# One decoder layer in one kernel: high-part and low-part matmuls in separate runs

## The chip, the cores and the metric

The kernel runs on one core of a Trainium2 chip. A core has five engines that run side by side, each with its own instruction queue. TensorE (PE) multiplies matrices: a weight load puts a stationary 128x128 tile into its array, and a matmul then streams a moving tile of up to 512 columns past it and adds the products into a bank of PSUM, the accumulator memory. VectorE (DVE), ScalarE (ACT) and GpSimd (POOL) do elementwise work; SyncE (SP) issues transfers between memory (HBM) and the on-chip SBUF. The metric is the time of one execution in device microseconds, as a median over several executions. The profile shows one of them.

## The reference

One layer of a hybrid decoder over 256 tokens with 2048 features, all in float32. What matters here are its projections:

- `u = rmsnorm(h)`, then `u @ w_in` with 12,320 columns: the gate z (2048), the state-space part x, B and C (4096), its step dt (32), and q, k and v of the attention (6144);
- a causal convolution, a chunked state-space scan and a gated norm on the first part; attention with three dilations on the second;
- `concat(ssd, attention) @ w_out` (4096 to 2048), a norm and the residual;
- `w_down` of `relu(u @ w_up)^2` (2048 to 8192 and back), a norm and the residual.

The result needs nearly float32 precision, so the kernel splits each operand x into a rounded high part hi and the rest lo = x - hi, and a product a * b becomes a_hi * b_hi + a_hi * b_lo + a_lo * b_hi.

## The kernel before

A product takes its weights in blocks of KB = 2 rows of 128 by NB = 512 columns. `weights` fetches a block into a tile `raw` by a transfer from SyncE (L136), has ACT write its high part into a tile `hi` (L125) and DVE the rest into a tile `lo` (L126). There are BUFS = 5 buffers each of `hi` and `lo` and four of `raw`; the whole of it runs under a high priority, so that blocks are prepared ahead.

There are two forms of product.

- *[token, feature]* (`gemm_tokens`): the activations are stationary, the weight block's 512 columns stream. Three matmuls for each 128 tokens and 128 rows: L187 (high, high), L188 (high activation, low weight), L189 (low activation, high weight). It makes z, v, w_out, w_down and the first block of w_up.
- *[feature, token]* (`gemm_features`, with `products`): 128x128 pieces of the weight block are stationary and the activations stream. The activations lie in `u2`, where for each 128 features the high parts of the 256 tokens (`uh`) and their low parts (`ul`) are neighbours. So one matmul of the weight's high piece streams 512 columns, high and low activation together (L201), and one of the weight's low piece streams the 256 high columns only (L202). The second adds into the first half of the same PSUM bank.

A [feature, token] product makes 512 features: four banks `acc[0]` to `acc[3]`, one for 128 features, and eight blocks over the 2048 rows. In each block there are four features times two row pieces, so eight pairs of an L201 and an L202, in the order of the list given to `products`: feature by feature, and within one by row piece. Each pair is one high matmul and the low matmul of the same piece. Behind a block, `pump` lets the next bit of waiting side work (a state-space group, an attention head, a piece of hidden activations) issue its instructions.

Behind the product, `added` takes the banks out in the order of the features: ACT copies a bank's second half (L219), DVE adds the first half to it (L220). There are six banks for such accumulators, so a product that follows another has two free ones for its first two features.

Thirty products go through `gemm_features`: seven for x, B and C, eight for q and k, fifteen for w_up. The first block of B is made by `first_block`, which calls `products` itself, once for each of the 16 row pieces with the four features as list, with the transposes of x (L276) set between; its order is written out by hand, the rest is ordered by priorities.

Instructions on an engine run in their order, so the order in which `products` emits its matmuls is TensorE's own order, but for high-priority side work set between them.

Of the kernel before, what the change touches and what calls it, by code (L numbers as in the profile page):

```python
# [16 lines left out]
P = 128  # L17
# [3 lines left out]
NK = D // P  # L21
# [18 lines left out]
KB = 2  # L40
# [31 lines left out]
def hymba_layer(ctx: ExitStack, tc: tile.TileContext, x, norm_mix_pre, w_in, conv_w, conv_b, dt_bias, a_log,  # L72
                d_skip, ssm_norm_w, w_out, norm_mix_post, norm_mlp_pre, w_up, w_down, norm_mlp_post,
                consts, out):
    nc = tc.nc
# [14 lines left out]
    u2 = big.tile([P, NK, 2, S], F32R, name="u2")  # L90
    uh, ul = u2[:, :, 0], u2[:, :, 1]
# [53 lines left out]
    def weights(src, k0, c0):  # L145

        with tc.high_priority(offset=AHEAD):
            raw = fetch(src, k0, c0)
            hi, lo = parts()
            with ExitStack() as order:  # L150
                while behind:
                    order.enter_context(tc.issue_after(behind.pop().ins))
                split(hi, lo, raw)
        return hi, lo
# [4 lines left out]
    def pump(n=1):  # L159
        for _ in range(n):  # L160
            if waiting:
                work = waiting.popleft()
                if next(work, work) is not work:
                    waiting.append(work)
# [5 lines left out]
    def gemm_tokens(src, c0, acts, nk, lag=0, at_end=None, pumps=1):  # L170


        acc = [bank() for _ in range(NT)]
        held = {}
        n = nk // KB
        for i in range(n + lag):
            if i < n:
                held[i] = weights(src, i * KB, c0)
            for t, at in ((0, i), (1, i - lag)):
                if not 0 <= at < n:  # L180
                    continue
                hi, lo = held[at]
                ts = slice(t * P, (t + 1) * P)
                for j in range(KB):
                    k = at * KB + j
                    a_h, a_l, r = acts(k)
                    nc.tensor.matmul(acc[t], a_h[:, r, ts], hi[:, j], start=k == 0, stop=False)  # L187
                    nc.tensor.matmul(acc[t], a_h[:, r, ts], lo[:, j], start=False, stop=False)  # L188
                    nc.tensor.matmul(acc[t], a_l[:, r, ts], hi[:, j], start=False, stop=k == nk - 1)  # L189
                if at == n - 1 and at_end:  # L190
                    at_end(t, acc[t])
            pump(pumps)
        return acc

    def features():
        return [bank().rearrange("p (b s) -> p b s", b=2) for _ in range(4)]

    def products(acc, hi, lo, k0, order):
        for f, j in order:
            k, fs = k0 + j, slice(f * P, (f + 1) * P)  # L200
            nc.tensor.matmul(acc[f], hi[:, j, fs], u2[:, k], start=k == 0, stop=False, skip_group_check=True)  # L201
            nc.tensor.matmul(acc[f][:, 0], lo[:, j, fs], uh[:, k], start=False, stop=k == NK - 1,  # L202
                             skip_group_check=True)

    def gemm_features(src, c0):


        acc = features()
        for k0 in range(0, NK, KB):
            hi, lo = weights(src, k0, c0)  # L210
            products(acc, hi, lo, k0, [(f, j) for f in range(4) for j in range(KB)])
            pump()
        return acc

# [72 lines left out]
    def first_block():  # L287
# [22 lines left out]
        for k0 in range(0, NK, KB):  # L310
            k1, k2 = k0 + KB, k0 + 2 * KB
            if k2 < NK:
                load_x(k2)
                load(k2)
            elif k2 == NK:
                load_parameters()
            products(acc, hi, lo, k0, [(f, 0) for f in range(4)])
            if k1 < NK:
                q = turn_x(k1)
            products(acc, hi, lo, k0, [(f, 1) for f in range(4)])  # L320
            if k1 == NK:
                break
            hi, lo = parts()
            if k1 >= FINE:
                part(k1, hi, lo, slice(0, KB))
            for f in range(KB):
                behind[:] = split_x(k1, q, f)
                if k1 < FINE:
                    part(k1, hi, lo, slice(f, f + 1))
            if k0 >= 4:  # L330
                squares(k0 // KB - 2)
# [103 lines left out]
    def conv_block(c0, ft0, acc=None):  # L435

        acc = acc or gemm_features(w_in, c0)
        dst = mp.tile([P, 4, S], F32, name="cT", bufs=5)
        for b in range(2):
            added(dst[:, 2 * b:2 * b + 2], acc[2 * b:2 * b + 2])  # L440
        for b in range(2):
            pad = sp1.tile([P, 2, S + 3], F32, name="pad", bufs=2)
            nc.gpsimd.memset(pad[:, :, 0:3], 0.0)
            nc.vector.tensor_tensor(pad[:, :, 3:], dst[:, 2 * b:2 * b + 2], rbc[:, None, :].to_broadcast([P, 2, S]),
                                    op=ALU.mult)
            for f in range(2):
                ft = ft0 + 2 * b + f
                d = dst[:, 2 * b + f]
                nc.vector.tensor_scalar(d, pad[:, f, 3:], cw[:, 3, ft:ft + 1], None, op0=ALU.mult)
                for w in (2, 1, 0):  # L450
                    nc.vector.scalar_tensor_tensor(d, pad[:, f, w:w + S], cw[:, w, ft:ft + 1], d,
                                                   op0=ALU.mult, op1=ALU.add)
                nc.scalar.activation(d, d, AF.Silu, bias=cb[:, ft:ft + 1])
        return dst
# [130 lines left out]
    def queries(c0, scale):  # L585
        acc = gemm_features(w_in, c0)
        dst = mp.tile([P, 4, S], F32, name="cT", bufs=5)
        for b in range(2):
            d = dst[:, 2 * b:2 * b + 2]
            added(d, acc[2 * b:2 * b + 2])  # L590
            nc.vector.tensor_tensor(d, d, scale[:, None, :].to_broadcast([P, 2, S]), op=ALU.mult)
        return dst

    for hb in range(4):
# [10 lines left out]
        acc = gemm_tokens(w_in, COL_V + hb * NB, act_u, NK)  # L605
# [60 lines left out]
    acc = gemm_tokens(w_out, 0, part, 2 * NK)  # L666
# [9 lines left out]
    for n in range(4):  # L676
        if n:
            acc = gemm_tokens(w_out, n * NB, part, 2 * NK, *((LAG_OUT, done, 2) if n == 3 else ()))
# [24 lines left out]
    acc = gemm_tokens(w_up, 0, act_u, NK, LAG_UP, None, 2)  # L703
# [20 lines left out]
    for hf in range(2):  # L724
        for fb in range(8):
            if hf == 0 and fb == 0:
                continue
            acc = gemm_features(w_up, hf * 4096 + fb * NB)
            for b in range(2):
                r = hp.tile([P, 2, S], F32, name="r", bufs=2)  # L730
                added(r, acc[2 * b:2 * b + 2])
                nc.vector.scalar_tensor_tensor(r, r, 0.0, rbc[:, None, :].to_broadcast([P, 2, S]),
                                               op0=ALU.max, op1=ALU.mult)
                hidden(4 * fb + 2 * b, r)
        for n in range(4):
            cs = slice(n * NB, (n + 1) * NB)
            last = hf == 1 and n == 3
            acc = gemm_tokens(w_down[hf * 4096:(hf + 1) * 4096], n * NB, part, 2 * NK,
                              *((LAG_DOWN, finish) if last else ()))
            for t in range(0 if last else NT):  # L740
                if hf == 0:
                    nc.scalar.activation(mw[:, t, cs], acc[t], AF.Copy)
                else:
                    nc.vector.tensor_add(mw[:, t, cs], acc[t], mw[:, t, cs])
                    junk = hp.tile([P, NB], BF16, name="junk", bufs=2)
                    nc.scalar.activation(junk, mw[:, t, cs], AF.Square, accum_out=ssq[:, t, n:n + 1])
                    nc.gpsimd.tensor_mul(mw[:, t, cs], mw[:, t, cs], wpost2[:, cs])
            if hf == 1 and n == 2:
                first3 = [sums_but_last(ssq, t) for t in range(NT)]
# [23 lines left out]
```

## Time and profile before

| what | value |
|---|---|
| median of 3 executions | 1516.53 us (1516.21 to 1521.23) |
| the profiled execution | 1517.63 us |
| its span, first to last instruction | 1515.8 us |
| PE busy | 1501.6 us, 99% of the span, 7725 matmuls |
| DVE busy | 914.5 us, 60% |
| ACT busy | 760.5 us, 50% |
| DMA | 283.13 MB, 187 GB/s on average |
| granted TensorE clock, mean | 0.998 |

The profiled execution's own time is 1.83 us longer than its span: that is what lies before its first and behind its last instruction. Busy is the time in which an engine worked on at least one instruction. Matmuls overlap in their pipeline, so one lasts longer than its distance to the next; what a matmul costs in a stream is read from the starts of matmuls in the timeline, and not from its duration. Weight loads (PEld) run beside matmuls.

### The profile page before, as it was taken

The numbers are of one execution on the slowest core, as the hardware profiler recorded it, in microseconds if no ns is written. First come the engines' busy times: TensorE is split into PE (matmuls) and PEld (weight loads), VectorE is DVE, ScalarE is ACT, GpSimd is POOL, SyncE is SP. The second block draws the span as 40 slices with busy tenths as digits, with TensorE's granted clock in tenths as the row PEclk, the third lists the DMA queues.
The fourth block names the chain that finished last, engine by engine and source line by source line (L and its number), as shares of the span: only waits on it lengthen the run. The fifth ranks groups of instructions, "written<-read, shape, count | busy, mean of one in ns | idle before, by whom it ended". The sixth has DMA issues, their size and how long they took to land.

```text
span 1515.8 us, 20167 instructions
## 1 busy us (share of the span) xinstructions
PE 1501.6 (99%) x7725; PEld 1277.5 (84%) x7725; DVE 914.5 (60%) x1314; ACT 760.5 (50%) x1065; POOL 56.7 (4%) x73
## 2 busy tenths in 40 slices
PE   9999999999999999999999999999999999999997
PEld 8888888888888888888878888888888888888885
DVE  5888897876555555544457656644444665555544
ACT  6575575554545454534456555543444555544432
POOL 0002200220000000000000000000000000000000
PEclk9999999999999999999999999999999999999999
DMA  7665666556665665576556666666566767655553
GB/s 256 195 210 180 182 181 194 177 157 181 169 178 169 175 171 174 169 267 193 185 166 215 187 183 187 187 194 194 193 192 187 191 184 187 187 193 193 192 172 125
DMA packets 147842, 283.13 MB, mean 187 GB/s; under 512 B 11313, under 2 KB 14241, under 8 KB 147233
## 3 DMA queue, kind: packets, MB, share of 16 engines
q1 hardware_dynamic: 143312, 272.37, 60.1%
q10 hardware_dynamic: 4432, 9.48, 1.8%
q8 instruction: 60, 0.98, 0.3%
q14 instruction: 38, 0.30, 0.1%
HBM read 279.68 MB, written 2.13 MB: 186 GB/s over the span
## 4 chain that ended last, share of the span: by engine, by line
PE 97%; DMA 1%; DVE 1%; issue 0%; ACT 0%; POOL 0%; POOLq 0%; DVEq 0%; SPq 0%; ACTq 0%
PE acc L201 30%; PE acc L187 16%; PE acc L189 16%; PE acc L188 16%; PE acc L202 15%; PE ps L516 1%; PE ps L559 0%; PE ps L581 0%; DMA raw_dt<-in_w_in_dram 0%; DMA raw<-in_w_in_dram 0%; DMA xs<-in_x_dram 0%; PE ps L472 0%; PE ps L582 0%; PE ps L558 0%; DVE h L646 0%
## 5 line engine op out<-in xcount | busy, mean ns | idle before, releaser
L126 DVE TENSOR_TENSOR lo<-raw,hi 128x1024 fp32r<-128x1024 f32 (+1 forms) x514 | 630.5, 1228 | 530.2 <-ACT hi L125 521.2
L125 ACT ACTIVATE hi<-raw 128x1024 fp32r<-128x1024 f32 (+1 forms) x514 | 542.1, 1056 | 651.0 <-PE acc L189 333.5
L201 PE MATMUL acc<-u,hi 128*128 128x512 f32 x1984 | 713.5, 403 | 0.0
L202 PE MATMUL acc<-u,lo 128*128 128x256 f32 x1984 | 557.2, 281 | 0.0
L201 PEld LDWEIGHTS acc<-u,hi 128*128 128x128 f32 x1984 | 373.5, 188 | 88.8 <-issue 0.2
L202 PEld LDWEIGHTS acc<-u,lo 128*128 128x128 f32 x1984 | 375.4, 189 | 1.2 <-DVE lo L126 0.3
L187 PE MATMUL acc<-hi,sh 128*128 128x512 f32 x384 | 150.6, 392 | 0.0
L187 PE MATMUL acc<-hi,ah 128*128 128x512 f32 x384 | 149.9, 390 | 0.0
L189 PE MATMUL acc<-hi,sl 128*128 128x512 f32 x384 | 149.5, 389 | 0.0
L188 PE MATMUL acc<-lo,sh 128*128 128x512 f32 x384 | 149.4, 389 | 0.0
L189 PE MATMUL acc<-hi,al 128*128 128x512 f32 x384 | 149.4, 389 | 0.0
L188 PE MATMUL acc<-lo,ah 128*128 128x512 f32 x384 | 149.4, 389 | 0.0
L187 PE MATMUL acc<-hi,u 128*128 128x512 f32 x288 | 113.0, 393 | 0.3 <-ACT u L127 0.3
L189 PE MATMUL acc<-hi,u 128*128 128x512 f32 x288 | 112.1, 391 | 0.7 <-DVE u L128 0.7
L188 PE MATMUL acc<-lo,u 128*128 128x512 f32 x288 | 112.0, 390 | 0.0
L189 PEld LDWEIGHTS acc<-hi,sl 128*128 128x128 f32 x384 | 72.1, 188 | 15.2
L189 PEld LDWEIGHTS acc<-hi,al 128*128 128x128 f32 x384 | 72.1, 188 | 15.0
L188 PEld LDWEIGHTS acc<-lo,ah 128*128 128x128 f32 x384 | 72.1, 188 | 14.9
L188 PEld LDWEIGHTS acc<-lo,sh 128*128 128x128 f32 x384 | 72.1, 188 | 14.9
L187 PEld LDWEIGHTS acc<-hi,sh 128*128 128x128 f32 x384 | 72.1, 188 | 14.8
L187 PEld LDWEIGHTS acc<-hi,ah 128*128 128x128 f32 x384 | 72.1, 188 | 14.7
L187 PEld LDWEIGHTS acc<-hi,u 128*128 128x128 f32 x288 | 54.1, 188 | 12.6 <-ACT u L127 1.5
(190 smaller groups left out, 941.0 us busy)
## 6 DMA issues: line engine op xcount, KB each, us to landing
raw<-in_w_in_dram SPq DMA_DIRECT2D x190, 512.0 KB, 3.7
raw<-in_w_up_dram SPq DMA_DIRECT2D x128, 512.0 KB, 3.8
raw<-in_w_down_dram SPq DMA_DIRECT2D x128, 512.0 KB, 3.6
raw<-in_w_out_dram SPq DMA_DIRECT2D x64, 512.0 KB, 4.3
bc<-acs_d ACTq DMA_DIRECT2D x8, 512.0 KB, 4.4
xs<-in_x_dram SPq DMA_DIRECT2D x8, 256.0 KB, 6.0
h<-in_x_dram ACTq DMA_DIRECT2D x1, 2048.0 KB, 11.7
raw<-in_w_in_dram SPq DMA_DIRECT2D x4, 256.0 KB, 5.1
```

The lines of the kernel that those rows point to most:

```text
L125: return (nc.scalar.activation(hi, src, AF.Copy), nc.vector.tensor_tensor(lo, src, hi.bitcast(F32), op=ALU.subtract))
L126: nc.vector.tensor_tensor(lo, src, hi.bitcast(F32), op=ALU.subtract))
L187: nc.tensor.matmul(acc[t], a_h[:, r, ts], hi[:, j], start=k == 0, stop=False)
L188: nc.tensor.matmul(acc[t], a_h[:, r, ts], lo[:, j], start=False, stop=False)
L189: nc.tensor.matmul(acc[t], a_l[:, r, ts], hi[:, j], start=False, stop=k == nk - 1)
L201: nc.tensor.matmul(acc[f], hi[:, j, fs], u2[:, k], start=k == 0, stop=False, skip_group_check=True)
L202: nc.tensor.matmul(acc[f][:, 0], lo[:, j, fs], uh[:, k], start=False, stop=k == NK - 1, skip_group_check=True)
L516: nc.tensor.matmul(p[:, c, r], bc[:, r, c * P:(c + 1) * P], xdt[:, c, r], start=True, stop=True)
```

## The change

`products` goes through its list twice: first all high-part matmuls (512 columns), then all low-part ones (256 columns). Its caller `gemm_features` chooses how long the list is. In the six middle blocks of the eight it passes all four features at once, so eight high matmuls come in one run and then eight low ones. In the first and the last block it calls `products` once for each feature, with two row pieces, so that each feature has two high matmuls and then two low ones. `first_block` is not edited, but its calls now make runs of four and four.

```diff
     def products(acc, hi, lo, k0, order):
+
         for f, j in order:
-            k, fs = k0 + j, slice(f * P, (f + 1) * P)
-            nc.tensor.matmul(acc[f], hi[:, j, fs], u2[:, k], start=k == 0, stop=False, skip_group_check=True)
-            nc.tensor.matmul(acc[f][:, 0], lo[:, j, fs], uh[:, k], start=False, stop=k == NK - 1,
+            nc.tensor.matmul(acc[f], hi[:, j, f * P:(f + 1) * P], u2[:, k0 + j], start=k0 + j == 0, stop=False,
                              skip_group_check=True)
+        for f, j in order:
+            nc.tensor.matmul(acc[f][:, 0], lo[:, j, f * P:(f + 1) * P], uh[:, k0 + j], start=False,
+                             stop=k0 + j == NK - 1, skip_group_check=True)
...
         for k0 in range(0, NK, KB):
             hi, lo = weights(src, k0, c0)
-            products(acc, hi, lo, k0, [(f, j) for f in range(4) for j in range(KB)])
+
+            edges = k0 in (0, NK - KB)
+            for fs in [(f,) for f in range(4)] if edges else [range(4)]:
+                products(acc, hi, lo, k0, [(f, j) for f in fs for j in range(KB)])
             pump()
```

The matmuls, their operands and their number are the same. In a middle block the first low piece is wanted eight matmuls after the first high one instead of one, and the last use of `hi` comes eight low matmuls before the block's end.

## The prediction

> **What bounds the kernel now.** I read the page first: who is busy, and what the chain that ended last is made of.
>
> ```profile
> span 1515.8 us, 20167 instructions
> PE 1501.6 (99%) x7725; PEld 1277.5 (84%) x7725; DVE 914.5 (60%) x1314; ACT 760.5 (50%) x1065; POOL 56.7 (4%) x73
> PE 97%; DMA 1%; DVE 1%; issue 0%; ACT 0%; POOL 0%; POOLq 0%; DVEq 0%; SPq 0%; ACTq 0%
> L126 DVE TENSOR_TENSOR lo<-raw,hi 128x1024 fp32r<-128x1024 f32 (+1 forms) x514 | 630.5, 1228 | 530.2 <-ACT hi L125 521.2
> L201 PE MATMUL acc<-u,hi 128*128 128x512 f32 x1984 | 713.5, 403 | 0.0
> L202 PE MATMUL acc<-u,lo 128*128 128x256 f32 x1984 | 557.2, 281 | 0.0
> L202 PEld LDWEIGHTS acc<-u,lo 128*128 128x128 f32 x1984 | 375.4, 189 | 1.2 <-DVE lo L126 0.3
> ```
>
> TensorE is busy 99% of the span and makes up 97% of the chain; the weight loads of low pieces waited for VectorE for 0.3 us in all. So there is no waiting in the [feature, token] products that a later use of `lo` could shorten. Only the rate at which matmuls follow each other can move the time. That rate is the distance between starts, since durations overlap (403 and 281 ns are longer than the distances below). So the second view is the timeline of matmuls, inside a w_up product without side work (start in us, duration, engine, line).
>
> ```profile
> 900.04 0.28 PE L202 MATMUL acc<-u,lo 128*128 128x256 f32 x1
> 900.16 0.40 PE L201 MATMUL acc<-u,hi 128*128 128x512 f32 x1
> 900.40 0.28 PE L202 MATMUL acc<-u,lo 128*128 128x256 f32 x1
> 900.52 0.40 PE L201 MATMUL acc<-u,hi 128*128 128x512 f32 x1
> 900.76 0.28 PE L202 MATMUL acc<-u,lo 128*128 128x256 f32 x1
> 900.87 0.40 PE L201 MATMUL acc<-u,hi 128*128 128x512 f32 x1
> 901.10 0.28 PE L202 MATMUL acc<-u,lo 128*128 128x256 f32 x1
> ```
>
> Three pairs take 901.10 - 900.04 = 1.06 us, or 353.3 ns a pair. Behind a low matmul the next start comes after 0.12, 0.12 and 0.11 us, behind a high one after 0.24, 0.24 and 0.23: on average 116.7 and 236.7 ns. The third view is the same timeline in a [token, feature] product, where every matmul streams 512 columns against a fresh 128x128 stationary tile, as a run of high matmuls would:
>
> ```profile
> 1400.03 0.39 PE L189 MATMUL acc<-hi,al 128*128 128x512 f32 x1
> ...
> 1406.83 0.39 PE L189 MATMUL acc<-hi,al 128*128 128x512 f32 x1
> ```
>
> Ten rounds of the three lines lie between, 30 matmuls in 6.80 us: 226.7 ns each. A matmul of 512 columns is thus 10 ns dearer where it alternates with one of 256 than where it follows its like. This is the whole room of the change, if the low matmuls do not give it back.
>
> **The change part by part.** Nothing is removed or added: 1984 high and 1984 low matmuls, each with its weight load, and the same transfers, splits and evacuations. What moves is order. Of the pairs, 30 products x 6 middle blocks x 8 = 1440 come into runs of eight, 30 x 2 end blocks x 8 = 480 into runs of two, and 64 of the first block into runs of four; the sum is the 1984 of the group's row.
>
> *Middle blocks, the high run.* Its lower end is the settled 226.7 ns. But eight are few, and the trace shows what 512-column matmuls do right behind the alternation, at the start of a w_down product that follows w_up:
>
> ```profile
> 976.36 0.28 PE L202 MATMUL acc<-u,lo 128*128 128x256 f32 x1
> 976.48 0.40 PE L187 MATMUL acc<-hi,sh 128*128 128x512 f32 x1
> 976.72 0.40 PE L188 MATMUL acc<-lo,sh 128*128 128x512 f32 x1
> 976.96 0.40 PE L189 MATMUL acc<-hi,sl 128*128 128x512 f32 x1
> 977.19 0.40 PE L187 MATMUL acc<-hi,sh 128*128 128x512 f32 x1
> ...
> 978.35 0.40 PE L189 MATMUL acc<-hi,sl 128*128 128x512 f32 x1
> ```
>
> From 976.48 to 978.35 there are eight (three rounds of the three lines, less one): 1.87 us, 233.8 ns each, and the first of them takes 0.24 us as in the alternation. The distance shrinks over a row of matmuls and not at once. That is the upper end. What comes behind a run of eight low matmuls no row shows; I take 232 ns, close to the upper end, because that row too begins behind a low matmul. Per matmul that is 4.7 ns less than 236.7.
>
> *Middle blocks, the low run.* The trace has no row of 256-column matmuls in a run with full 128x128 loads. The nearest is the dt product, 256 columns of the same `u`, run on run, with stationary tiles of half the width:
>
> ```profile
> 49.06 0.28 PE L384 MATMUL ps<-u,wdt 128*64 128x256 f32 x1
> ...
> 51.17 0.28 PE L384 MATMUL ps<-u,wdt 128*64 128x256 f32 x1
> 127.35 1.86 PEld L516 LDWEIGHTS ps<-xdt,bc 128*128 128x128 f32 x16
> 129.13 0.19 PEld L201 LDWEIGHTS acc<-u,hi 128*128 128x128 f32 x1
> ```
>
> Nine rounds of L384 and L385, 18 matmuls in 2.11 us: 117.2 ns each. The last two rows are weight loads of the full width behind each other, under matmuls of 64 columns that cannot fill the time: 16 in 1.78 us, 111.3 ns each. So a load every 117 ns is possible, though with little to spare, and though one load's record is 189 ns long. The lower end for a low run is 110 ns, the shorter of the distances shown above (0.11); the upper end is 120, the longest of them (0.12). I take the dt row's 117.2, 0.5 above the 116.7 of now.
>
> The sum for a pair in a middle block is 232 + 117.2 = 349.2 ns against 353.3: 4.1 ns less, and times 1440 it is 5.9 us. The ends are 226.7 + 110 = 336.7 (23.9 us less) and 233.8 + 120 = 353.8 (0.7 us more).
>
> One correction: the alternation is not at 353.3 everywhere. In a passage of the state-space stage it holds a faster rhythm:
>
> ```profile
> 79.97 0.40 PE L201 MATMUL acc<-u,hi 128*128 128x512 f32 x1
> ...
> 86.21 0.40 PE L201 MATMUL acc<-u,hi 128*128 128x512 f32 x1
> ```
>
> That is 18 pairs in 6.24 us, 346.7 ns. Where this holds, the runs save nothing (349.2 is 2.5 more). As an estimate, a third of the middle blocks of the seven x, B and C products is like this: 7 x 48 / 3 = 112 pairs x 6.6 ns = 0.7 us of the saving gone, which leaves 5.2 us.
>
> *End blocks.* Two high, two low: in the transition above, the first two 512-column distances are 976.72 - 976.48 = 0.24 and 976.96 - 976.72 = 0.24 us, which is the alternation's own price. I take nothing. For the range: two pairs cost 706.7 ns now, at most 2 x 240 + 2 x 120 = 720 (13 ns x 240 = 3.2 us more), at least what the middle's lower end gives, 673 (8.0 us less). The order of the features stays, so `added` finds its banks at the same times.
>
> *The first block* has 64 pairs in runs of four; at the middle's rate it is 0.3 us, which I leave out. Its first three banks end up to three high matmuls later (0.7 us); two spare banks carry the next product through its first two features, four pairs or 1.4 us, so I price this at nothing; without that cover it is 0.7 us, once.
>
> *Buffers.* `hi` is free eight low matmuls (0.94 us) earlier in a middle block, `lo` at the same time as now. The first low piece is wanted 8 x 232 ns = 1.9 us after the first high one instead of 0.24 us. Both loosen the preparation, on which TensorE hardly waits. VectorE's 1.23 us of splitting per block of 2.8 us (row L126) hides below the matmuls as before, and so does ScalarE's part. No wait is added, and nothing queues behind one. Side work is set between the same blocks.
>
> The profiled execution took 1517.6 us with 1515.8 of span and 1.8 outside; less 5.2 it is 1512.4. The median is 1.1 us below that execution, so I predict **1511.3 us** in the median's terms, 0.34% less.
>
> **The Trainium skill against this.** "TensorE: Matmul & The Clock Gate", section "Back-to-back issue gap", gives the gap of a matmul as its column count over the clock plus a constant, with no term for its neighbours. By that rule order costs nothing and the change does nothing; the trace speaks against it in part, as the same 512 columns take 226.7 ns in one place and 236.7 in the other.
>
> **The rivals.**
>
> *Order does not matter (no change, 1516.5 us).* The cost may belong to the short matmul: each of 256 columns may lay a fixed debt of 13 ns on the stream, and the next long one pays it. For it: in the transition the excess over 226.7 is paid over eight matmuls, (233.8 - 226.7) x 8 = 57 ns, though no short one came any more. Then a run of low matmuls would collect the debt, and the next high run pay it: 353.3 as before. Against: the rhythm at 346.7 shows that the same pairs can go faster. The skill's rule above ends at the same time.
>
> *The runs settle at once (about 1501 us).* The settled 226.7 with 117.2 is 343.9, 9.4 less; x 1440 = 13.5 us, and a fifth of that per pair in the end blocks, 480 x 1.9 = 0.9 us, with 0.7 taken back for the fast passages: 13.7, so 1516.5 - 13.7 = 1502.8; with low matmuls at 113 it would be 1497. For it: the neighbours within a run are all alike. Against: the slow settling in the transition.
>
> *Low runs wait for their weight loads (slower, about 1528 us).* Now every second load has a 512-column matmul to lie under. In a low run each of eight loads has only 117 ns, and the record of one is 189 ns long. If loads under 256 fp32r columns come at 130 ns, a pair is 232 + 130 = 362, 8.7 more; x 1440 = 12.5 us, 1529. If a load could only begin when the one before had ended, at 189 ns, it would be 232 + 189 - 353.3 = 67.7 x 1440 = 97 us. It decides from 353.3 - 232 = 121.3 ns per low matmul on. Against: 16 full loads in a row at 111.3 ns. For: those lay under 64-column matmuls of another type. The skill's page on TensorE, section "LDWEIGHTS (loading the stationary operand)", has 128 columns load in an estimated 107 ns; the 111.3 of this trace is near it.
>
> *The edit does not do what it says:* side work with a higher priority could split the runs, but it is set between blocks now and takes no more places than before; this would land at no change and is counted there.
>
> **How the numbers follow.** From 0.5% on (7.6 us) a measurement of this kernel can tell a change from none: below 1508.9 is faster, above 1524.1 slower. The forecast (1506 to 1515, by 230 to 233.8 for a high and 115 to 119 for a low matmul) has a chance of 0.38, and about a third of it lies beyond 0.5%; no influence of order 0.25; settling at once 0.27, all of it faster; waiting loads 0.10, nearly all slower. So faster 0.13 + 0.27 = 0.40, slower 0.09, the same 0.51. The range from 1498 to 1522 holds the forecast, no change and nearly all of the settled case, and leaves out the waiting loads (0.10) and the lower ends of the low run (0.08). Cases of gain and of no change hold most of it; the likeliest one's own range is 1506 to 1515.
>
> **What would show it.** In the timeline after: a run of eight L201 whose first distance is about 0.24 us and whose mean is near 232 ns, then eight L202 at about 117 ns; a middle block of 2.79 us instead of 2.83. High runs at 227 ns from the first on speak for settling at once; a first run of eight whose surplus equals what the low run saved speaks for the debt; L202 distances above 121 ns show waiting loads. Idle time on TensorE behind `lo` L126 or at L201 that is more than a few us in all would mean that my reading of the buffers is wrong. The prediction fails if end blocks cost more than 720 ns for two pairs, or if the rhythm of runs depends on what went before as the two rhythms of the alternation do.

## The result and the profile after

The changed kernel took 1508.89 us (median of 6, 1508.5 to 1512.54) beside 1517.25 us of the kernel before (median of 6): a ratio of 0.9944 with a 95% interval from 0.9928 to 0.9959. Run a second time, beside one of the experiments below, it gave 1509.32 us and 0.9950 [0.9936, 0.9963]. So it is 7 to 8 us faster, at and just beyond the bound of 0.5% that the prediction set. The forecast was 1511.3, a gain of 5.2 us. The granted clock is 0.998 in both profiles.

The page after, in the lines that answer to those quoted of before:

```profile
span 1507.1 us, 20168 instructions
PE 1493.2 (99%) x7725; PEld 1275.4 (85%) x7725; DVE 917.5 (61%) x1314; ACT 763.1 (51%) x1063; POOL 56.1 (4%) x73
PE 96%; DVE 2%; DMA 1%; ACT 1%; issue 1%; SPq 0%; POOL 0%; POOLq 0%; DVEq 0%; ACTq 0%
L201 PE MATMUL acc<-u,hi 128*128 128x512 f32 x1984 | 539.3, 398 | 1.3 <-DVE u L128 1.2
```

The same 7725 matmuls, TensorE still at 99%, and the span 8.7 us shorter. The low matmul's line is now L204. The first reading is the timeline inside a w_up product: one middle block. A row holds a whole run here (its start, how long it was busy, the line, the count).

```profile
1172.77 2.00 PE L201 MATMUL acc<-u,hi 128*128 128x512 f32 x8
1174.61 1.11 PE L204 MATMUL acc<-u,lo 128*128 128x256 f32 x8
1175.56 0.40 PE L201 MATMUL acc<-u,hi 128*128 128x512 f32 x1
```

Eight high matmuls take 1174.61 - 1172.77 = 1.84 us, 230 ns each, and eight low ones 0.95 us, 118.8 each. The block takes 2.79 us, the figure that the prediction had added up from 232 and 117.2; before it took 8 x 353.3 ns = 2.83 us. The chain of waits of the same kernel (start, share of the chain in us, line, count) shows an end block and a first block behind each other, and then middle blocks:

```profile
1164.56 0.47 PE acc L201 x2
1165.03 0.23 PE acc L204 x2
...
1170.13 1.84 PE acc L201 x8
1171.97 0.95 PE acc L204 x8
...
1178.52 1.84 PE acc L201 x8
```

From 1164.56 to 1170.13 there are 16 pairs in runs of two: 348.1 ns each. From 1170.13 to 1178.52 there are three middle blocks, 24 pairs: 349.6 ns, in these rounded rows. Runs of two are no dearer than runs of eight. The prediction had put them at the alternation's price.

Where the time came from is read from the same places of both programs: the first transpose behind the first block, the first matmul of w_out, and both ends of the eight w_up products of the second half. First before:

```profile
34.59 0.27 PE L263 MATMUL ps<-cst,rows 64*128 64x64 f32 x1
607.19 0.39 PE L187 MATMUL acc<-hi,sh 128*128 128x512 f32 x1
1150.62 0.39 PE L201 MATMUL acc<-u,hi 128*128 128x512 f32 x1
1331.51 0.40 PE L187 MATMUL acc<-hi,sh 128*128 128x512 f32 x1
```

and after:

```profile
32.82 0.27 PE L268 MATMUL ps<-cst,rows 64*128 64x64 f32 x1
603.27 0.39 PE L187 MATMUL acc<-hi,sh 128*128 128x512 f32 x1
1144.88 0.62 PE L201 MATMUL acc<-u,hi 128*128 128x512 f32 x2
1323.52 0.40 PE L187 MATMUL acc<-hi,sh 128*128 128x512 f32 x1
```

The lead is 1.77 us at the end of the first block, 3.92 at w_out, 5.74 at the second half's w_up products and 7.99 behind them. So the fifteen products with w_in give 2.15 us (0.43 of them in the first one, which holds waits of the start) and the stretch from w_out on, with fifteen w_up products, 4.07. The remaining 0.7 of the 8.7 us of span lie behind the last matmul, in the end of the program (10.4 us in the profile of before, 9.6 after), and no run tells why. The eight w_up products of the second half went from (1331.51 - 1150.62) / 512 = 353.3 ns a pair to 178.64 us / 512 = 348.9. The first 1.77 us cannot be put down to the rate of matmuls: an experiment below with the old first block ends it at 32.97.

### The profile page after: what moved, and what is told of

The parts are those of the page before. It is cut to its first block, busy times and chain, and to the rows that moved or that the text cites. A ratio compares the mean times of both kernels' runs of the same rounds, so it can differ in the third digit from the quotient of the medians.

```text
span 1507.1 us, 20168 instructions
## 1 busy us (share of the span) xinstructions
PE 1493.2 (99%) x7725; PEld 1275.4 (85%) x7725; DVE 917.5 (61%) x1314; ACT 763.1 (51%) x1063; POOL 56.1 (4%) x73
## 4 chain that ended last, share of the span: by engine, by line
PE 96%; DVE 2%; DMA 1%; ACT 1%; issue 1%; SPq 0%; POOL 0%; POOLq 0%; DVEq 0%; ACTq 0%
PE acc L201 29%; PE acc L187 16%; PE acc L188 16%; PE acc L189 16%; PE acc L204 15%; PE ps L521 1%; DMA raw<-in_w_in_dram 1%; DVE lo L126 1%; PE ps L564 0%; PE ps L586 0%; ACT hi L125 0%; DMA raw_dt<-in_w_in_dram 0%; PE ps L477 0%; PE ps L563 0%; PE ps L587 0%
## 5 line engine op out<-in xcount | busy, mean ns | idle before, releaser
L201 PE MATMUL acc<-u,hi 128*128 128x512 f32 x1984 | 539.3, 398 | 1.3 <-DVE u L128 1.2
L201 PEld LDWEIGHTS acc<-u,hi 128*128 128x128 f32 x1984 | 344.8, 189 | 51.4 <-DVE u L128 1.4
L204 PEld LDWEIGHTS acc<-u,lo 128*128 128x128 f32 x1984 | 296.2, 189 | 36.9
L204 PE MATMUL acc<-u,lo 128*128 128x256 f32 x1984 | 305.4, 281 | 0.0
```

The source lines that it names most:

```text
L201: nc.tensor.matmul(acc[f], hi[:, j, f * P:(f + 1) * P], u2[:, k0 + j], start=k0 + j == 0, stop=False, skip_group_check=True)
L204: nc.tensor.matmul(acc[f][:, 0], lo[:, j, f * P:(f + 1) * P], uh[:, k0 + j], start=False, stop=k0 + j == NK - 1, skip_group_check=True)
```

## The experiments

**Which part gives the gain.** One kernel has the new order in the first block alone, one everywhere but there. Both edits are shown against the changed kernel.

```diff
 e1_first_block_only, gemm_features:
-            edges = k0 in (0, NK - KB)
-            for fs in [(f,) for f in range(4)] if edges else [range(4)]:
-                products(acc, hi, lo, k0, [(f, j) for f in fs for j in range(KB)])
+            paired(acc, hi, lo, k0, [(f, j) for f in range(4) for j in range(KB)])
 e2_first_block_as_before, first_block (paired is the products of before):
-            products(acc, hi, lo, k0, [(f, 0) for f in range(4)])
+            paired(acc, hi, lo, k0, [(f, 0) for f in range(4)])
...
-            products(acc, hi, lo, k0, [(f, 1) for f in range(4)])
+            paired(acc, hi, lo, k0, [(f, 1) for f in range(4)])
```

> Only the first block groups its high and low matmuls in fours; all other products alternate high and low as before. The profile after showed the first high matmul 1.6 us earlier than before (5.77 against 7.38 us). Theory rate (the gain is the distance between matmuls, and the earlier start is chance of the first transfers): 64 pairs times about 4 ns, 0.3 us, so 1517 us, ratio 0.999 to 1.000. Theory start (the earlier start is the edit's doing, as the first low piece is wanted later): 1.6 us less, ratio about 0.9985 to 0.999, and the first transposes of x early in every profile.

> The first block alternates high and low as before; the thirty other products have the runs of the change. Theory rate: nearly all of the gain, ratio 0.994 to 0.996. Theory start: 1.6 us of the 8 are missing, ratio 0.9955 to 0.9965.

Measured: the first 1515.79 us, ratio 0.9989 [0.9980, 0.9998]; the second 1511.94 us, 0.9966 [0.9954, 0.9979]. The ratios lie at or near those given for the theory of the start, but not for its reason: the first high matmul comes at 6.23 us in the profile of the first and at 6.32 in that of the second, which has the old order there, so the early start does not hang on the edit. In the profile of the second, the first block alternates as before and yet ends early, and then TensorE waits longer (first a row of the timeline, then two of the view of waits in the stretch from 30 to 62 us: us in total, times, longest):

```profile
32.97 0.27 PE L275 MATMUL ps<-cst,rows 64*128 64x64 f32 x1
```

```profile
PE ps L366 <- DVE dg L365: 2.9, 1, 2.9
...
ACT wdt L125 <- DMA raw_dt<-in_w_in_dram: 2.6, 1, 2.6
```

The first block ends at 32.97 against 32.82 in the changed kernel. The 34.59 of before came with a first high matmul at 7.38 us, behind a transfer of x for which TensorE had waited 0.7 us in that execution (5.77 us and no such wait in the changed kernel's). TensorE's wait for `dg` (the row of L366) was 0.8 us in the profile of before, 0.5 in that of the changed kernel, 2.9 here, and the profile of the first experiment shows none. The old first block alone does not bring it: it was 0.9 us in the run with breaks below, which has that block too. It stands at `over_partitions`, where VectorE scales the identity for TensorE; VectorE's queue holds the split of the dt weights ahead of it, which waits for ScalarE, which waits for their transfer (2.6 us in this profile). The edits also move VectorE's own order: here and in the changed kernel a weight split of 1.23 us stands between the two, in the kernel before and in the first experiment it does not.

The profiles say where each kernel loses or gains. The second one reaches the first block's successor at 33.26 us and the next product at 65.37, the changed kernel at 33.11 and 61.37: 3.85 us more for that one product, 2.4 of them in this wait. From there to w_out they are alike (541.87 and 541.90 us). The first one keeps the slower rate of before in w_up (353.3 ns a pair in the second half), so its 1.45 us in the median come from elsewhere; its profile leads that of before by 3.19 us at that next product (60.38 against 63.57) and by 3.0 at the end. So the order in the first block seems to be worth more than the rate of its 64 pairs (0.3 us), through waits near it, though the interval of the 1.45 us (0.3 to 3.0) just reaches that. The two halves of the change, 1.5 and 5.3 us, add up to 6.7 and leave 0.7 to 1.6 us of the whole (7.4 and 8.4 in its two measurements) open. That this wait separates the medians, too, is read from one profile of each and not shown.

**How long must a run be?** All eight blocks go feature by feature, two high and two low.

```diff
 e3_runs_of_two and e10_runs_of_two_again:
-            edges = k0 in (0, NK - KB)
+            edges = True
```

> All eight blocks go feature by feature: two high, two low, no run of eight anywhere. My forecast took end blocks at the alternation's price (353.3 ns a pair), since the settling takes several matmuls: then the gain is gone but for the first block, 1516 us. The end blocks of the profile after show otherwise: 469 + 229 + 463 + 233 ns for four pairs, 348.5 ns a pair, against (1841 + 953) / 8 = 349.2 in middle blocks. By that row runs of two are worth as much as runs of eight: 1440 x 0.7 ns = 1 us less than after, 1508 us, ratio 0.9935 to 0.9945.

> Runs of two in every block once more, beside the kernel with the fast rhythm on the same chip: 1507 us, ratio 0.992 to 0.995.

Measured: 1507.26 us, 0.9934 [0.9922, 0.9947], and in a second measurement of it 1506.69 us, 0.9931 [0.9918, 0.9943]. Its chain of waits:

```profile
1166.09 0.46 PE acc L201 x2
...
1171.66 0.46 PE acc L201 x2
```

16 pairs lie between, 348.1 ns each. The simplest form of the change does at least as well as the one made. That a run must be long to gain, on which the forecast for end blocks rested, is wrong.

**Sixteen of a kind.** Every second middle block takes its low matmuls first.

```diff
 e6_runs_of_sixteen:
-                products(acc, hi, lo, k0, [(f, j) for f in fs for j in range(KB)])
+                products(acc, hi, lo, k0, [(f, j) for f in fs for j in range(KB)],
+                         not edges and k0 // KB % 2 == 0)
 in products, the two loops as functions:
+        for part in (low, high) if low_first else (high, low):
+            part()
```

> As after, but every second middle block takes its low matmuls first, so that the runs of neighbouring blocks join to sixteen of a kind. Theory settling (a pair costs 226.7 + 120 = 346.7 ns in any order, and each change from one kind to the other costs a few matmuls of settling): in the profile after, a run of eight high ones takes 1841 ns, 27 more than 8 x 226.7, and one of eight low ones 953, 7 less than 8 x 120, so 20 ns a block. With half as many changes 10 ns a block, 180 blocks, 1.8 us less than after: 1507 us. Theory runs of two are best for another reason (short runs): slower than after.

> The changed kernel once more, beside the runs of sixteen on the same chip: 1509 us, ratio 0.993 to 0.996. The wait of TensorE at the end of the first block for the transposed scale (0.5 us in the profile after, 0.8 in that of before, 2.7 to 2.9 in two of the experiments) depends on when the small transfer of the dt weights lands, and may differ.

Measured: 1508.79 us, 0.9946 [0.9934, 0.9959], beside 1509.32 us of the changed kernel. In its chain of waits:

```profile
1172.35 1.91 PE acc L207 x16
1174.27 3.65 PE acc L202 x16
1177.92 1.91 PE acc L207 x16
```

A low and a high run of sixteen take 5.57 us, 348.1 ns a pair, 1.1 to 1.5 below runs of eight, as the settling would have it. The expectation was 10 ns a block, 0.06 us a product. In the profiles the eight w_up products of the second half take 178.17 us here and 178.64 in the changed kernel measured beside it, 0.06 us less each, so there the size is met. The whole is only 0.5 us faster instead of 1.8, within what these intervals can tell; the profile has 1.3 us of the wait behind the first block against 0.4 in that of the changed kernel. So the size is confirmed in the stretch and not in the time.

**Is it the neighbour in the bank?** High and low alternate one by one, but the low matmul comes two pieces later, so neighbours share neither a PSUM bank nor a piece of weights. The edit is shown with its helper written out in place; the two low matmuls left over at a product's end follow behind its last block.

```diff
 e4_low_two_later (alternation as before, first block as before):
-                products(acc, hi, lo, k0, [(f, j) for f in fs for j in range(KB)])
+            for f, j in [(f, j) for f in range(4) for j in range(KB)]:
...
+                late.append((f, lo[:, j, fs], k0 + j))
+                if len(late) > 2:
+                    low(acc, *late.popleft())
```

> High and low still alternate one by one, but each low matmul comes two pieces later than its high one, so that neighbours never add into the same bank and never belong to the same piece of weights. Theory length (what costs is that a matmul of 512 columns stands beside one of 256): 353.3 ns a pair as before, 1516 to 1517 us, ratio 0.999 to 1.001. Theory bank (what costs is that the low matmul adds into the bank that the high one is still adding into): about 346 ns a pair or less, 7 ns x 1900 = 13 us less, ratio 0.991.

Measured: 1514.03 us, 0.998 [0.9971, 0.9989]: neither. The timeline says why. Here are two w_up products behind each other (starts of high matmuls; each dotted line hides 20 further ones):

```profile
1176.84 0.39 PE L217 MATMUL acc<-u,hi 128*128 128x512 f32 x1
...
1184.12 0.40 PE L217 MATMUL acc<-u,hi 128*128 128x512 f32 x1
1198.72 0.40 PE L217 MATMUL acc<-u,hi 128*128 128x512 f32 x1
...
1206.14 0.40 PE L217 MATMUL acc<-u,hi 128*128 128x512 f32 x1
```

21 pairs in 7.28 us are 346.7 ns, and 21 pairs in 7.42 us are 353.3. The same instructions in the same order ran at two rates, in one kernel (the two products lie in other banks and buffers, but a run below has both rates within one product). So it is not the bank; and it is not simply that unequal neighbours cost more. The alternation has two rhythms, and one of them costs as little as the settled runs: 226.7 + 120 = 346.7.

**What sets the rhythm?** The kernel before, with one break in the alternation in the third and one in the sixth block of every w_up product; behind a break the pairs alternate again. `kick` gives 2, 3, 4, 8 or "s" in turn in those two blocks, and nothing elsewhere.

```diff
 e5_kicks, against the kernel before:
-            products(acc, hi, lo, k0, [(f, j) for f in range(4) for j in range(KB)])
+            n = kick(src, k0)
+            if n == "s":
+                ordered(acc, hi, lo, k0, pieces, "hllh")
+            elif n:
+                ordered(acc, hi, lo, k0, pieces, "h" * n + "l" * n)
+            else:
+                products(acc, hi, lo, k0, pieces)
```

> The kernel before, but in the fifteen w_up products the alternation is broken once in the third and once in the sixth block: in turn two high and two low, three and three, four and four, eight and eight, or high low low high; behind it the pairs alternate as before. Theory two rhythms (the alternation holds one of two rhythms, 346.7 or 353.3 ns a pair, that is set by the place where it is entered and kept from then on): behind a break the pairs run at one of these two, and the same break out of the same rhythm leads to the same one each time. In the run with low matmuls two pieces later, 48 pairs took 16.64 us in some w_up products and 16.96 in others, which is these two. Theory width (unequal neighbours always cost the same): 353.3 behind every break.

Measured: 1513.92 us, a single execution. A part of its timeline, with a break of four and four and one of eight and eight:

```profile
1181.08 0.40 PE L201 MATMUL acc<-u,hi 128*128 128x512 f32 x1
...
1184.26 0.40 PE L201 MATMUL acc<-u,hi 128*128 128x512 f32 x1
1184.61 1.09 PE L211 MATMUL acc<-u,hi 128*128 128x512 f32 x4
1185.54 0.63 PE L213 MATMUL acc<-u,lo 128*128 128x256 f32 x4
...
1187.40 0.39 PE L201 MATMUL acc<-u,hi 128*128 128x512 f32 x1
...
1198.15 0.39 PE L201 MATMUL acc<-u,hi 128*128 128x512 f32 x1
1198.49 2.01 PE L211 MATMUL acc<-u,hi 128*128 128x512 f32 x8
1200.35 1.11 PE L213 MATMUL acc<-u,lo 128*128 128x256 f32 x8
...
1201.64 0.40 PE L201 MATMUL acc<-u,hi 128*128 128x512 f32 x1
...
1202.70 0.40 PE L201 MATMUL acc<-u,hi 128*128 128x512 f32 x1
```

Before the first break 9 pairs take 3.18 us, 353.3 ns each. Behind it 31 pairs take 10.75 us, 346.8, over the boundary between two products. Behind the second it is 353.3 again (3 pairs in 1.06 us). Outside the first w_up product, into which side work is set, every stretch ran at one of the two values and kept it to the next break. From the slower rhythm a break of four led to the faster one each of the five times it came; from the faster one a break of eight led to the slower one each of five times. A break of two out of the slower rhythm led to either, against the expectation that the same break leads to the same rhythm. The slower rhythm has a cycle of three pairs: by the starts in the trace they take 240 + 120, 236 + 114 and 232 + 118 ns, 1060 in all. The two breaks of two that led to the faster rhythm came behind a pair of 232 + 118, the two that did not behind one of 240 + 120. With this place taken in, the 18 breaks there out of the slower rhythm make nine cases, and each of the seven cases that came more than once led to the same rhythm every time.

**Does the width make it?** The alternation of before, but the low matmul streams 512 columns too. The product of the two low parts is then added to the sum, which the kernel otherwise leaves out.

```diff
 e7_low_as_wide, against the kernel before:
-            nc.tensor.matmul(acc[f][:, 0], lo[:, j, fs], uh[:, k], start=False, stop=k == NK - 1,
+            nc.tensor.matmul(acc[f], lo[:, j, fs], u2[:, k], start=False, stop=k == NK - 1,
```

> The kernel before with its alternation, but the low matmul streams all 512 columns of the activations (high and low, so it also adds the product of the two low parts). Theory fixed price (a matmul costs 0.2083 us for each 500 columns, by 226.7 - 120 = 106.7 ns for 256, and 13.3 ns on top, and the slow rhythm needs unequal widths): 226.7 ns for each, 453.3 a pair, 100 ns more than 353.3, 1984 pairs, 1715 us. Theory tile (a change between the tiles hi and lo is what costs): 236.7 each, 473.3 a pair, 1755 us.

Measured: 1718.08 us, a single execution. In its timeline

```profile
1364.64 0.39 PE L201 MATMUL acc<-u,hi 128*128 128x512 f32 x1
...
1366.00 0.39 PE L201 MATMUL acc<-u,hi 128*128 128x512 f32 x1
```

are three pairs in 1.36 us, 453.3 each, as the fixed price has it. A change between `hi` and `lo` tiles costs nothing here, and with equal widths no slower rhythm shows.

**Holding the faster rhythm.** Runs of two where side work keeps breaking the order (w_in), and in w_up the plain alternation of before, with three breaks set where the run with kicks had shown them to lead into the faster rhythm.

```diff
 e9_fast_rhythm:
+            if src is w_in:
+                for f in range(4):
+                    products(acc, hi, lo, k0, [(f, j) for j in range(KB)])
+            else:
+                ordered(acc, hi, lo, k0, pieces, {(0, 4): "hhll", (0, 10): "hhhlll", (7, 4): "hllh"}.get((n, k0), ""))
```

> Runs of two in all products with w_in, the first block as after; in the w_up products high and low alternate one by one, as before, and three breaks are set where such breaks led into the fast rhythm in the run with kicks: two and two, then three and three in the first w_up product, high low low high in the first of the second half. Theory two rhythms: the alternation then stays at 346.7 ns a pair to the end of each half, 16.64 us for the 48 pairs of a product's middle, against 16.72 in runs of two, 16.76 in the change and 16.96 before; 13 products x 0.11 us = 1.4 us less than runs of two alone, about 1506 us, ratio 0.992 to 0.994. Theory runs (only like neighbours are cheap): 353.3 ns a pair in w_up, 15 x 0.32 = 4.8 us more than runs of two, 1512 us.

Measured: 1505.66 us, 0.9925 [0.9911, 0.9938], beside 1506.69 us of runs of two. In its timeline, in the fourth w_up product of the second half:

```profile
1212.64 0.39 PE L213 MATMUL acc<-u,hi 128*128 128x512 f32 x1
...
1224.78 0.39 PE L213 MATMUL acc<-u,hi 128*128 128x512 f32 x1
```

35 pairs in 12.14 us, 346.9 ns: single alternation, which cost 353.3 before, at a lower price than any of the runs. The eight w_up products of the second half take 177.61 us in this profile, 178.34 in that of runs of two measured beside it, and 180.89 in that of before. This kernel is the fastest of all here by the median, and its interval and that of runs of two overlap. What carries the point is the timeline, and that the rhythm came out where it was foretold.

## Why the prediction was right, and where it was not

*What bounds the kernel.* Right for the products: TensorE's rate. The later need for `lo` and the earlier release of `hi` bought nothing that the profile shows; the low pieces' loads had waited 0.3 us to begin with. "No wait is added" does not quite hold: in the first block a high matmul waits 1.2 us for the low part of u (the row of L201 above), which no high matmul did in the profile of before. The waits near the first block, where the prediction saw nothing, are also where the first two experiments found their microseconds.

*The middle blocks.* Right in sum, by two small misses that cancel, which is luck: 230 ns instead of 232 for a high matmul, 118.8 instead of 117.2 for a low one; 2.79 us a block as forecast. The low run was read from the dt product, whose stationary tiles are half as wide; the run's 120 ns of e6 (1.91 us for sixteen) shows the row that it should have been, the upper end.

*The correction for passages that were already at 346.7 ns* was too small. The products with w_in gave 2.15 us in all, those with w_up 4.07, though each group has fifteen; so 1.9 us are missing with w_in, where the prediction took off 0.7. In the trace of before about 180 pairs of the x, B and C products stand in the faster rhythm, not 112, which makes 1.2 us at 6.6 ns each. Four of these products, with the most side work in them, gained nothing (their 64 pairs took 23.27 to 23.30 us each before, 23.27 to 23.28 after, from starts to next starts). The rest of the shortfall stays open.

*The end blocks* are the term that failed: "I take nothing", since the distances right behind the alternation were 0.24 us. They run at about 348.5 ns (the rows above: 348.1), so 16 pairs x 4.8 = 0.08 us a product, which with 48 x 4.1 = 0.20 us makes the 0.27 us that a w_up product gained (4.07 / 15). The rows that I took the price from show a stream that comes out of the slower rhythm, and not one of runs.

*The first block* was priced at nothing. Alone it gave 1.45 us in the median (by its interval 0.3 to 3.0). The rate of its 64 pairs was to be 0.3 by the prediction; the rest, as far as the profiles tell, are waits near it. The profiles of before and after differ by 1.77 us at its end, most of it in the start of the first high matmul. It is why the size of the step from 1517 to 1509 should not be read off two profiles alone: 6.2 us of the 8.7 are in the products, the rest lies ahead of and behind them.

*The sum.* The prediction took 5.2 us for the products and the two profiles show 6.2. That these are near each other is partly luck: the end blocks gave 0.08 us a product, an estimated 2.3 us over thirty, where nothing was taken, and the products with w_in fell 1.2 us further short than was taken off for them. The first block's 1.45 us stood in no term.

*The rivals.* "Order does not matter", with a debt of each low matmul that the next high ones pay, fell: the same matmuls cost 353.3, 349, 348 and 346.7 ns a pair by order and by history. The Trainium skill's rule that speaks for it ("TensorE: Matmul & The Clock Gate", section "Back-to-back issue gap": columns over the clock plus a constant) is given there for an isolated matmul and not for a stream with weight loads. Settled runs here can be written in its form, with 106.7 ns for 256 columns and 13.3 ns on top, though two widths cannot test a form; that rule misses what the alternation does. "Settle at once" fell for the high runs, which average 230 ns over eight. "Low runs wait for their loads" fell: 120 ns each in runs of sixteen, below the 121.3 from which it would have cost.

*The cause* was wrong. I read the 10 ns between 236.7 and 226.7 as the price of an unequal neighbour, with a few matmuls of settling. The runs with the low matmul two pieces later, with breaks and with the held rhythm show a stream of unequal pairs that has two stable rhythms, 6.7 ns apart, of which the kernel before had settled in the dear one in all of w_up. The prediction had the other one in a row of its own (346.7), but took it for a passage to subtract. The change helps as it leaves the dear rhythm, and it pays something for its own changes between high and low (1.84 us for eight high matmuls against 8 x 226.7 ns = 1.81), though not in proportion to their number, as runs of two show. What in TensorE makes the two rhythms these runs do not tell.

## What to carry to other kernels

Read the distance between starts, not busy time, when an engine is at 99%: a stream can be full and still run 2% slow. Add up what each matmul costs in a settled stream of its like; where the stream at hand costs more, reorder it, and try the smallest reordering first (runs of two did what runs of eight did). A rhythm depends on what went before it, so a row taken from a transition prices the transition, and a gain that hangs on a rhythm should be looked up again in the timeline after every edit ahead of it.

## What the runs showed of the hardware

- A stream of alternating matmuls of 512 and 256 fp32r columns with a fresh 128x128 load each ran at 346.7 or 353.3 ns a pair in the w_up products of these runs. It kept its rhythm over product boundaries (512 pairs at 353.3 in the kernel before) and changed it there only where the order was broken; the kind of break and its place in a cycle of three pairs went together with the rhythm that followed.
- In settled runs of one width a matmul took 226.7 ns for 512 columns and 120 for 256 (1.91 us for sixteen): 106.7 ns per 256 columns and 13.3 ns for each matmul, which gives the 346.7 of the faster rhythm and the 453.3 of two wide ones.
- Sixteen low matmuls in a row, each with a load of 128 columns whose own record lasts 189 ns, came every 120 ns.
